# A decoder block's start reordered: small rows in ScalarE's queue, GpSimd's powers beside PSUM reads, the second row block turned in one go

## The chip, the cores and the metric

The kernel runs on one core of a Trainium2 chip. A core has five engines with a queue of instructions each: TensorE (PE in the profile; its weight loads are PEld), VectorE (DVE), ScalarE (ACT), GpSimd (POOL) and SyncE (SP), which only issues transfers here. Times are device microseconds (us) of one execution.

## The reference, cut to what matters

One layer over 512 tokens with 2048 features, all in float32:

```
h = rmsnorm(x, g_mix);  z = h @ w_in        # [conv B|C|V, attn Q|K|V, forget logits, two gates]
conv branch, forgetting attention, gated merge, x = x + merged @ w_mix_out
h = rmsnorm(x, g_mlp);  x = x + relu(h @ w_ff1)**2 @ w_ff2
out = rmsnorm(x, g_final)

rmsnorm(x, g) = x * rsqrt(mean(x*x) + 1e-6) * g
```

The change touches only the very start: the first `rmsnorm` and the first two of the products that make z.

## The kernel before, in words

**Products.** Every large product is done by a Strassen-like scheme on 2 x 2 blocks with seven block products, named A11, A12, S1 to S4 and A22. Each float32 operand is split into a high part (`high_of`, line 110, ScalarE, rounded to a 32-bit format that TensorE takes at full rate) and a low part (`low_of`, line 113, VectorE, the difference of the two). A block product is high x high, low x high and high x low: in `mm_rows` the lines 183, 185 and 187, in `mm_cols` the lines 164, 166 and 168. Classes of columns of w_in are `Group`s; `ahead` (through `load`, line 221) sends for a quarter of their weights, 1 MB, into one of four slots x0 to x3. `gV0` makes the first 256 columns x 2 of V, `heads[1]` (called `keys`) the first two heads' keys and queries.

**The start.** The 512 rows of x come in four blocks of 128 (`load_rows`, line 605). The sum of squares of a row is made by ScalarE (`squares`, line 487), and its power -1/2 by GpSimd (lines 483 and 623). Then the block is turned so that features lie on the partitions. For blocks 1 and 2 `turn` (line 525) does it with a matrix product whose other operand is the identity times the row factor (`dgs`, lines 654 and 668); even feature chunks make A11, odd ones A12. VectorE reads the result from PSUM and multiplies it by g_mix (`gained`, line 533). Blocks 3 and 4 are scaled in place by their factors (lines 694 and 695) and turned in pairs by `turn_both` (line 541) and `gained_both` (lines 549 and 551). The vectors g_mix, g_mlp, b_gate and conv_w come as small rows (`rows`, lines 635 and 637), are transposed on TensorE (line 649) and copied to `cols` (line 655); `rows` uses the slot x3. TensorE is fed small products that nobody reads (`stay_awake`, line 611) while it has nothing else.

**What sets the order.** Where `strict[0]` is true, `tied` holds an instruction behind the one written before it on its engine, so the start runs in the written order on each engine; with `strict[0]` false again (line 708) a planner places instructions by priority and by its own estimate of when operands are ready. A tile's slot is given on when its last reader is done. The order of TensorE's work in the start is: fillers, transposition of the small rows, fillers, block 1 turned (even, odd), V's A11 for block 1, block 2's even half turned, V's A12 for block 1, block 2's odd half turned, V's A11 and A12 for block 2, the pair-wise turning of blocks 3 and 4, then the keys.

Of the kernel before, what the change touches and what calls it, by code (L numbers as in the profile page):

```python
# [8 lines left out]
F32 = mybir.dt.float32  # L9
F32R = mybir.dt.float32r  # L10
BF16 = mybir.dt.bfloat16
AF = mybir.ActivationFunctionType
ALU = mybir.AluOpType
AX = mybir.AxisListType

P = 128
S = 512
D = 2048
KT = D // P
# [3 lines left out]
CT = CW // P  # L23
# [3 lines left out]
EPS = 1e-6  # L27
# [18 lines left out]
def tile_hybrid_block(ctx: ExitStack, tc, x, g_mix, w_in, b_f, b_gate, conv_w, w_conv_out,  # L46
                      w_attn_out, w_mix_out, g_mlp, w_ff1, w_ff2, g_final, out):
    nc = tc.nc
    x, out = x[0], out[0]
# [4 lines left out]
    stat = ctx.enter_context(tc.tile_pool(name="stat", bufs=2))  # L54
# [8 lines left out]
    def bank(i, name):  # L63
        return psum.tile([P, S], F32, tag=f"p{i}", name=name)
# [24 lines left out]
    ident = const.tile([P, P], F32, name="ident")  # L89
    mhalf = const.tile([P, 1], F32, name="mhalf")  # L90
# [12 lines left out]
    def tied(i):  # L103

        if strict[0]:
            tc.keep_in_program_order(i)
        return i

    def high_of(src, hi):
        return tied(nc.scalar.activation(out=hi, in_=src, func=AF.Copy))  # L110

    def low_of(src, hi, lo):
        return tied(nc.vector.tensor_tensor(out=lo, in0=src, in1=hi.bitcast(F32), op=ALU.subtract))  # L113
# [365 lines left out]
    def rstd_of(part, both=False):  # L479
        v = stat.tile([P, 1], F32, tag="v", name="v")  # L480
        tied(nc.vector.tensor_reduce(out=v, in_=part, axis=AX.X, op=ALU.add))
        r = stat.tile([P, 1], F32, tag="r", name="r")
        nc.gpsimd.tensor_tensor(out=r, in0=v, in1=mhalf, op=ALU.pow)
        return (v, r) if both else r
# [82 lines left out]
    xin = [xp[t // 2][:, t % 2] for t in range(NT)]  # L567

    Q1 = Quarters(px, gmixT)

    def store_v(c0, w):
        def put(i, j, v):
            c = c0 + j * w
            n = min(w, AW - c)
            nc.gpsimd.dma_start(out=v_d[2 * i:2 * i + 2, :, c:c + n].rearrange("t p c -> p t c"), in_=v[:, :, :n])
            if n < w:
                add(fl[:, 2 * i:2 * i + 2, :], v[:, :, n:], bf.unsqueeze(1).to_broadcast([P, 2, NH]))
        return put
# [8 lines left out]
    gV0 = Group(w_in, COL_AV, COL_AV + VW, VW, Q1.moving, mm_rows, ((4,), (3,), (6,), (7,)), store_v(0, VW))  # L587

    def kq(hp, banks):
        return Group(w_in, COL_K + hp * HS, COL_Q + hp * HS, HS, Q1.moving, mm_cols, banks, store_kq(hp), QSCALE,  # L590
                     extra={"S3": "first"})
# [8 lines left out]
    heads = [gV0] + [kq(hp, ((a,), (3,), (6,), (7,))) for hp, a in enumerate((0, 1, 2, 5))]  # L600

    def load_rows(t, n, queues):
        w = D // n
        for i in range(n):
            tied(queues[i % len(queues)].dma_start(out=xin[t][:, i * w:(i + 1) * w],
                                                   in_=x[t * P:(t + 1) * P, i * w:(i + 1) * w]))

    def stay_awake(n):

        for i in range(n):  # L610
            tied(nc.tensor.matmul(awake[:, :P], ident, ident, start=True, stop=True))

    def squares(t, n):

        w = D // n
        for i in range(n):
            tied(square_part(xin[t][:, i * w:(i + 1) * w], ss1[:, t, i:i + 1], junk[:, i * w:(i + 1) * w]))

    def factor_of(t):

        v, r = (stat.tile([P, 1], F32, tag=f"{k}2", name=k) for k in "vr")
        nc.gpsimd.tensor_tensor(out=v, in0=ss1[:, t, 0:1], in1=ss1[:, t, 4:5], op=ALU.add)
        nc.gpsimd.tensor_tensor(out=r, in0=v, in1=mhalf, op=ALU.pow)
        return r

    both = pair(6, F32, "junk")
# [1 line left out]
    dgs = [both[:, 0, t * P:(t + 1) * P] for t in range(2)]  # L628
    ss1 = const.tile([P, NT, 5], F32, name="ss1")
    nc.vector.memset(ss1[:, :, 4:5], EPS)  # L630
    strict[0] = True
    rows = main.tile([NV, P], F32, tag="x3", name="rows")
    r0 = 0
    for src, n in ((g_mix[0], KT), (g_mlp[0], KT), (b_gate[0], 2 * KT)):
        tied(nc.gpsimd.dma_start(out=rows[r0:r0 + n, :], in_=src.rearrange("(k p) -> k p", p=P)))
        r0 += n
    tied(nc.gpsimd.dma_start(out=rows[r0:r0 + 3 * CT, :], in_=conv_w[0].rearrange("j (k p) -> (j k) p", p=P)))

    load_rows(0, 4, (nc.sync, nc.scalar))
    tied(nc.scalar.activation(out=warm, in_=warm, func=AF.Square))  # L640
    gV0.ahead(0, 0)
    load_rows(1, 2, (nc.sync,))
    gV0.ahead(1, 0)
    load_rows(2, 1, (nc.sync,))
    heads[1].ahead(0, 0)
    load_rows(3, 1, (nc.sync,))
    awake, pv = bank(3, "awake"), bank(7, "pv")
    stay_awake(12)
    tied(nc.tensor.transpose(pv[:, :NV], rows, ident[:NV, :NV]))
    stay_awake(6)  # L650
    heads[1].ahead(1, 0)

    squares(0, 4)
    tied(nc.vector.tensor_scalar(out=dgs[0], in0=ident, scalar1=rstd_of(ss1[:, 0, :]), scalar2=None, op0=ALU.mult))
    tied(nc.vector.tensor_copy(cols, pv[:, :NV]))
    even, odd = Q1.turn(0, 0, (0, 1)), Q1.turn(0, 1, (2, 5))
    hi1, lo1 = parts([P, KT // 2, VW])
# [3 lines left out]
    A11, A12 = (Q1.cut(n, 0) for n in ("A11", "A12"))  # L661
    high_of(*A11[:2])
    squares(1, 1)
    Q1.gained(0, 1, 0, odd[0])
    low_of(*A11)
    Q1.gained(0, 1, 1, odd[1])
    high_of(*A12[:2])
    tied(nc.scalar.activation(out=dgs[1], in_=ident, func=AF.Copy, scale=factor_of(1)))
    for h in range(2):
        qs = slice(h * KT // 4, (h + 1) * KT // 4)  # L670
        low_of(gV0.X[0, 0][:, qs], hi1[:, qs], lo1[:, qs])
    gV0.a, b = gV0.acc("a"), gV0.acc("b")
    mm_rows(gV0.a, Q1.moving("A11"), hi1, lo1, True, blocks=(0,))
    even = Q1.turn(1, 0, (6, 7))
    hi2, lo2 = parts([P, KT // 2, VW])
    high_of(gV0.X[1, 0], hi2)
    low_of(*A12)
    low_of(gV0.X[1, 0], hi2, lo2)
    mm_rows(b, Q1.moving("A12"), hi2, lo2, True, blocks=(0,))
    odd = Q1.turn(1, 1, (0, 1))  # L680
    squares(2, 1)
    for n in range(2):
        Q1.gained(1, 0, n, even[n])
    A11, A12 = (Q1.cut(n, 1) for n in ("A11", "A12"))
    high_of(*A11[:2])
    for n in range(2):
        Q1.gained(1, 1, n, odd[n])
    high_of(*A12[:2])
    low_of(*A11)
    low_of(*A12)  # L690
    mm_rows(gV0.a, Q1.moving("A11"), hi1, lo1, True, blocks=(1,))
    mm_rows(b, Q1.moving("A12"), hi2, lo2, True, blocks=(1,))
    squares(3, 1)
    tied(nc.vector.tensor_scalar(out=xin[2], in0=xin[2], scalar1=factor_of(2), scalar2=None, op0=ALU.mult))
    tied(nc.scalar.activation(out=xin[3], in_=xin[3], func=AF.Copy, scale=factor_of(3)))
    tied(nc.gpsimd.dma_start(out=bf, in_=b_f.to_broadcast([P, NH])))
    keys = heads[1]
    keys.ready["A11"] = hi3, lo3 = keys.places()
# [48 lines left out]
    for t in range(NT):  # L747
# [3 lines left out]
                            op0=ALU.mult)  # L751
# [22 lines left out]
    for b in range(3):  # L774
        nc.scalar.activation(out=sel[32 * b:32 * b + NH, :, :], in_=identb[0:NH, 0:NH].unsqueeze(2).to_broadcast([NH, NH, P]),
                             func=AF.Copy, scale=warm[0:NH, :])
# [119 lines left out]
    n = 0  # L896
# [253 lines left out]
    n = turns[0] + 1  # L1150
# [497 lines left out]
```

## Time and profile before

| what | us |
|---|---|
| median of 3 runs | 2447.67 |
| the runs | 2450.6, 2443.35, 2447.67 |
| the profiled execution | 2449.19 |
| its span, first to last instruction | 2447.5 |

In the profile, a line of a timeline has the start in us from the span's start, the duration (of a merged group, from its first start to its last end), the engine, the line of the kernel, the operation, output and input by the program's names, the shapes and the count; in brackets stands the idle time of the engine before it and what ended it. An engine name with q (SPq) is its queue, where transfers are issued. A float32 product of the fillers and of the turnings leaves two records each. A table of stretches has one row per stretch with the busy time of each engine, the clock that TensorE was granted as a share of the full one, and the share of the transfer engines' time that was used.

### The profile page before, as it was taken

The page shows a single profiled execution, that of the slowest core. Times are in us where ns is not written, and L with a number is a line of the kernel's source. Part 1 is how long each engine was busy: PE and PEld are TensorE (multiplying, and loading weights), DVE is VectorE, ACT ScalarE, POOL GpSimd, SP SyncE. Part 2 cuts the span into 40 slices and gives each one's busy share as a digit, 9 for nine tenths or more (in the row PEclk, how much of TensorE's full clock was granted, in tenths as well). Part 3 has the DMA queues.
Part 4 walks back from the last instruction along what each step waited for, and adds up shares of the span by engine and source line. Part 5 has one row for each costly group of instructions (what it writes and reads, how often), then busy time and mean ns, then how long its engine had stood idle before and what let it go on. Part 6 is the DMA issues. An engine that isn't in the chain of part 4 may idle for free.

```text
span 2447.5 us, 41525 instructions
## 1 busy us (share of the span) xinstructions
PE 2412.4 (99%) x17804; PEld 2268.2 (93%) x17804; DVE 2042.7 (83%) x1711; ACT 1206.3 (49%) x1232; POOL 281.3 (11%) x453
## 2 busy tenths in 40 slices
PE   8999999999999999999999999999999999999998
PEld 8999899999999999899999999999997888888886
DVE  6987777788888778888889898898978888889898
ACT  6444433344555445355656666666655333333334
POOL 1100000111121111113300000000011001100000
PEclk9999999999999999999999999999999999999999
DMA  7564544445656664657855655646587576655763
GB/s 251 168 194 148 153 135 148 141 145 178 206 169 210 209 221 151 228 156 257 302 194 180 229 196 201 234 175 229 199 303 274 168 243 228 236 193 178 248 226 101
DMA packets 283785, 489.87 MB, mean 200 GB/s; under 512 B 11669, under 2 KB 195057, under 8 KB 283217
## 3 DMA queue, kind: packets, MB, share of 16 engines
q1 hardware_dynamic: 232624, 278.48, 36.2%
q0 software_dynamic: 50112, 207.17, 22.8%
q8 instruction: 139, 2.28, 0.4%
q10 hardware_dynamic: 864, 1.57, 0.2%
q14 instruction: 46, 0.37, 0.0%
HBM read 377.60 MB, written 109.05 MB: 199 GB/s over the span
## 4 chain that ended last, share of the span: by engine, by line
PE 88%; DVE 5%; DMA 3%; issue 2%; ACT 1%; POOL 1%; DVEq 0%; SPq 0%; POOLq 0%; ACTq 0%
PE a L168 6%; PE a L164 6%; PE a L166 6%; PE a L185 5%; PE a L183 5%; PE a L187 5%; PE d L164 5%; PE d L168 5%; PE d L166 5%; PE c L164 4%; PE c L166 4%; PE c L168 4%; PE d L187 3%; PE d L185 3%; PE d L183 3%; PE b L168 2%
## 5 line engine op out<-in xcount | busy, mean ns | idle before, releaser
L110 ACT ACTIVATE th<-x 128x2048 fp32r<-128x2048 f32 (+1 forms) x280 | 537.4, 1920 | 516.3 <-DVE x L124 174.8
L113 DVE TENSOR_TENSOR tl<-x,th 128x2048 fp32r<-128x2048 f32 (+2 forms) x281 | 638.8, 2279 | 164.5 <-ACT th L110 149.4
L124 DVE TENSOR_TENSOR x<-x,x 128x2048 f32<-128x2048 f32 (+1 forms) x160 | 365.6, 2285 | 24.1 <-DMA x<-in_w_in_dram 20.2
L110 ACT ACTIVATE th<-y 128x2048 fp32r<-128x2048 f32 (+1 forms) x109 | 185.7, 1704 | 273.8 <-PE a L185 138.6
L113 DVE TENSOR_TENSOR tl<-y,th 128x2048 fp32r<-128x2048 f32 (+1 forms) x109 | 218.9, 2013 | 29.5 <-ACT th L110 27.9
L183 PE MATMUL a<-th,us 128*128 128x512 f32 x512 | 199.3, 389 | 1.9 <-ACT th L110 1.9
L185 PE MATMUL a<-th,us 128*128 128x512 f32 x512 | 199.2, 389 | 0.0
L164 PE MATMUL c<-S,th 128*128 128x256 f32 x848 | 196.3, 277 | 0.6 <-ACT th L110 0.6
L166 PE MATMUL c<-S,th 128*128 128x256 f32 x848 | 195.9, 277 | 0.0
L164 PE MATMUL a<-S,th 128*128 128x256 f32 x784 | 182.3, 278 | 0.8 <-ACT th L110 0.8
L166 PE MATMUL a<-S,th 128*128 128x256 f32 x784 | 180.8, 276 | 0.0
L164 PEld LDWEIGHTS c<-S,th 128*128 128x128 f32 x848 | 159.3, 188 | 1.0 <-ACT th L110 0.7
L166 PEld LDWEIGHTS c<-S,th 128*128 128x128 f32 x848 | 159.3, 188 | 0.0
L164 PEld LDWEIGHTS a<-S,th 128*128 128x128 f32 x784 | 147.2, 188 | 1.0 <-ACT th L110 1.0
L166 PEld LDWEIGHTS a<-S,th 128*128 128x128 f32 x784 | 147.3, 188 | 0.0
L187 PE MATMUL a<-tl,us 128*128 128x512 f32 x512 | 136.9, 389 | 0.6 <-DVE tl L113 0.6
L166 PE MATMUL b<-A,th 128*128 128x256 f32 x544 | 126.9, 278 | 0.0
L164 PE MATMUL b<-A,th 128*128 128x256 f32 x544 | 126.9, 278 | 0.0
L164 PE MATMUL a<-A,th 128*128 128x256 f32 x544 | 126.5, 278 | 0.0
L166 PE MATMUL a<-A,th 128*128 128x256 f32 x544 | 126.4, 277 | 0.0
L164 PE MATMUL d<-S,th 128*128 128x256 f32 x544 | 126.3, 278 | 0.0
L166 PE MATMUL d<-S,th 128*128 128x256 f32 x544 | 125.8, 277 | 0.0
(393 smaller groups left out, 6081.6 us busy)
## 6 DMA issues: line engine op xcount, KB each, us to landing
x<-in_w_in_dram SPq DMA_DIRECT2D x86, 1024.0 KB, 5.9
y<-in_w_ff_dram SPq DMA_DIRECT2D x64, 1024.0 KB, 7.6
x<-in_w_ff_dram SPq DMA_DIRECT2D x60, 1024.0 KB, 8.3
us<-s_d POOLq DMA_DIRECT2D x48, 1024.0 KB, 9.4
s_d<-rh POOLq DMA_DIRECT2D x32, 896.0 KB, 5.1
s_d<-r POOLq DMA_DIRECT2D x32, 896.0 KB, 5.6
x<-in_w_mix_out_dram SPq DMA_DIRECT2D x17, 1024.0 KB, 6.7
g_d<-o POOLq DMA_DIRECT2D x32, 256.0 KB, 2.9
```

Source lines behind the costliest of these rows:

```text
L110: return tied(nc.scalar.activation(out=hi, in_=src, func=AF.Copy))
L113: return tied(nc.vector.tensor_tensor(out=lo, in0=src, in1=hi.bitcast(F32), op=ALU.subtract))
L124: return nc.vector.tensor_tensor(out=out, in0=a, in1=b, op=ALU.subtract)
L164: nc.tensor.matmul(o, hi[:, q, js], Sh, start=first and q == 0 and j == 0, stop=False, skip_group_check=True)
L166: nc.tensor.matmul(o, hi[:, q, js], Sl, start=False, stop=False, skip_group_check=True)
L168: nc.tensor.matmul(o, lo[:, q, js], Sh, start=False, stop=q == nq - 1, skip_group_check=True)
L183: tied(nc.tensor.matmul(o, Sh, hi[:, q, :], start=begin and q == 0, stop=False, skip_group_check=True))
L185: tied(nc.tensor.matmul(o, Sl, hi[:, q, :], start=False, stop=False, skip_group_check=True))
L187: tied(nc.tensor.matmul(o, Sh, lo[:, q, :], start=False, stop=q == nq - 1, skip_group_check=True))
```

## The change

- The first block's rows are issued by SyncE alone, in four pieces, and first of all; the small rows are issued by ScalarE instead of GpSimd.
- The rows of block 4 are issued ahead of the keys' weights, and both quarters of the keys' weights follow directly.
- One filler more stands behind the transposition of the small rows.
- Row factors: the addition of epsilon moves from GpSimd to VectorE (`mean_of`), and GpSimd does the power alone (`factor`), written so that VectorE's next instruction reads PSUM. Block 1's power is now tied too.
- In VectorE's order half of the low part of V's first weights moves ahead of block 2's factor, and block 1's second odd gain behind it; ScalarE makes block 2's factor matrix before A12's high part.
- Block 2's odd half is turned directly behind its even half, ahead of V's A12 for block 1.
- Block 2's even gains move ahead of the low part of V's second weights; its A11 is split completely before its odd gains; the squares of block 4 move ahead of them, and the factors and scalings of blocks 3 and 4 ahead of the last split.

```diff
--- before.py
+++ after.py
@@ -616,11 +616,16 @@
         for i in range(n):
             tied(square_part(xin[t][:, i * w:(i + 1) * w], ss1[:, t, i:i + 1], junk[:, i * w:(i + 1) * w]))
 
-    def factor_of(t):
-
-        v, r = (stat.tile([P, 1], F32, tag=f"{k}2", name=k) for k in "vr")
-        nc.gpsimd.tensor_tensor(out=v, in0=ss1[:, t, 0:1], in1=ss1[:, t, 4:5], op=ALU.add)
-        nc.gpsimd.tensor_tensor(out=r, in0=v, in1=mhalf, op=ALU.pow)
+    def mean_of(t):
+
+        v = stat.tile([P, 1], F32, tag="vf", name="v", bufs=4)
+        tied(nc.vector.tensor_scalar(out=v, in0=ss1[:, t, 0:1], scalar1=EPS, scalar2=None, op0=ALU.add))
+        return v
+
+    def factor(v):
+
+        r = stat.tile([P, 1], F32, tag="rf", name="r", bufs=4)
+        tied(nc.gpsimd.tensor_tensor(out=r, in0=v, in1=mhalf, op=ALU.pow))
         return r
 
     both = pair(6, F32, "junk")
@@ -629,29 +634,30 @@
     ss1 = const.tile([P, NT, 5], F32, name="ss1")
     nc.vector.memset(ss1[:, :, 4:5], EPS)
     strict[0] = True
+    load_rows(0, 4, (nc.sync,))
     rows = main.tile([NV, P], F32, tag="x3", name="rows")
     r0 = 0
     for src, n in ((g_mix[0], KT), (g_mlp[0], KT), (b_gate[0], 2 * KT)):
-        tied(nc.gpsimd.dma_start(out=rows[r0:r0 + n, :], in_=src.rearrange("(k p) -> k p", p=P)))
+        tied(nc.scalar.dma_start(out=rows[r0:r0 + n, :], in_=src.rearrange("(k p) -> k p", p=P)))
         r0 += n
-    tied(nc.gpsimd.dma_start(out=rows[r0:r0 + 3 * CT, :], in_=conv_w[0].rearrange("j (k p) -> (j k) p", p=P)))
-
-    load_rows(0, 4, (nc.sync, nc.scalar))
+    tied(nc.scalar.dma_start(out=rows[r0:r0 + 3 * CT, :], in_=conv_w[0].rearrange("j (k p) -> (j k) p", p=P)))
     tied(nc.scalar.activation(out=warm, in_=warm, func=AF.Square))
     gV0.ahead(0, 0)
     load_rows(1, 2, (nc.sync,))
     gV0.ahead(1, 0)
     load_rows(2, 1, (nc.sync,))
+    load_rows(3, 1, (nc.sync,))
     heads[1].ahead(0, 0)
-    load_rows(3, 1, (nc.sync,))
+    heads[1].ahead(1, 0)
     awake, pv = bank(3, "awake"), bank(7, "pv")
     stay_awake(12)
     tied(nc.tensor.transpose(pv[:, :NV], rows, ident[:NV, :NV]))
-    stay_awake(6)
-    heads[1].ahead(1, 0)
+    stay_awake(7)
 
     squares(0, 4)
-    tied(nc.vector.tensor_scalar(out=dgs[0], in0=ident, scalar1=rstd_of(ss1[:, 0, :]), scalar2=None, op0=ALU.mult))
+    part = stat.tile([P, 1], F32, tag="vf", name="part", bufs=4)
+    tied(nc.vector.tensor_reduce(out=part, in_=ss1[:, 0, :], axis=AX.X, op=ALU.add))
+    tied(nc.vector.tensor_scalar(out=dgs[0], in0=ident, scalar1=factor(part), scalar2=None, op0=ALU.mult))
     tied(nc.vector.tensor_copy(cols, pv[:, :NV]))
     even, odd = Q1.turn(0, 0, (0, 1)), Q1.turn(0, 1, (2, 5))
     hi1, lo1 = parts([P, KT // 2, VW])
@@ -663,36 +669,38 @@
     squares(1, 1)
     Q1.gained(0, 1, 0, odd[0])
     low_of(*A11)
+    qs, rest = slice(0, KT // 4), slice(KT // 4, KT // 2)
+    low_of(gV0.X[0, 0][:, qs], hi1[:, qs], lo1[:, qs])
+    v = mean_of(1)
     Q1.gained(0, 1, 1, odd[1])
+    tied(nc.scalar.activation(out=dgs[1], in_=ident, func=AF.Copy, scale=factor(v)))
     high_of(*A12[:2])
-    tied(nc.scalar.activation(out=dgs[1], in_=ident, func=AF.Copy, scale=factor_of(1)))
-    for h in range(2):
-        qs = slice(h * KT // 4, (h + 1) * KT // 4)
-        low_of(gV0.X[0, 0][:, qs], hi1[:, qs], lo1[:, qs])
+    low_of(gV0.X[0, 0][:, rest], hi1[:, rest], lo1[:, rest])
     gV0.a, b = gV0.acc("a"), gV0.acc("b")
     mm_rows(gV0.a, Q1.moving("A11"), hi1, lo1, True, blocks=(0,))
-    even = Q1.turn(1, 0, (6, 7))
+    even, odd = Q1.turn(1, 0, (6, 7)), Q1.turn(1, 1, (0, 1))
     hi2, lo2 = parts([P, KT // 2, VW])
     high_of(gV0.X[1, 0], hi2)
     low_of(*A12)
+    for n in range(2):
+        Q1.gained(1, 0, n, even[n])
     low_of(gV0.X[1, 0], hi2, lo2)
     mm_rows(b, Q1.moving("A12"), hi2, lo2, True, blocks=(0,))
-    odd = Q1.turn(1, 1, (0, 1))
     squares(2, 1)
-    for n in range(2):
-        Q1.gained(1, 0, n, even[n])
     A11, A12 = (Q1.cut(n, 1) for n in ("A11", "A12"))
     high_of(*A11[:2])
+    low_of(*A11)
+    squares(3, 1)
+    r2 = factor(mean_of(2))
     for n in range(2):
         Q1.gained(1, 1, n, odd[n])
+    r3 = factor(mean_of(3))
     high_of(*A12[:2])
-    low_of(*A11)
+    tied(nc.vector.tensor_scalar(out=xin[2], in0=xin[2], scalar1=r2, scalar2=None, op0=ALU.mult))
+    tied(nc.scalar.activation(out=xin[3], in_=xin[3], func=AF.Copy, scale=r3))
     low_of(*A12)
     mm_rows(gV0.a, Q1.moving("A11"), hi1, lo1, True, blocks=(1,))
     mm_rows(b, Q1.moving("A12"), hi2, lo2, True, blocks=(1,))
-    squares(3, 1)
-    tied(nc.vector.tensor_scalar(out=xin[2], in0=xin[2], scalar1=factor_of(2), scalar2=None, op0=ALU.mult))
-    tied(nc.scalar.activation(out=xin[3], in_=xin[3], func=AF.Copy, scale=factor_of(3)))
     tied(nc.gpsimd.dma_start(out=bf, in_=b_f.to_broadcast([P, NH])))
     keys = heads[1]
     keys.ready["A11"] = hi3, lo3 = keys.places()
```

## The prediction

> **What bounds the kernel now.** I read the page's first and fourth parts, then the start by timeline, the waits of SP's queue, and a table of stretches laid on the grid on which the granted clock changes.
>
> ```profile
> PE 2412.4 (99%) x17804; PEld 2268.2 (93%) x17804; DVE 2042.7 (83%) x1711; ACT 1206.3 (49%) x1232; POOL 281.3 (11%) x453
> PE 88%; DVE 5%; DMA 3%; issue 2%; ACT 1%; POOL 1%; DVEq 0%; SPq 0%; POOLq 0%; ACTq 0%
> ```
>
> TensorE is busy for 99% of the span and holds 88% of the chain that ended last. Every edit lies before the pair-wise turning of row blocks 3 and 4 (line 541), so the question is how much earlier that stage starts, and whether what follows moves with it.
>
> ```profile
> 5.79:9.20 3.41, 1.53 (x14) 1.37 (x14) 0.75 (x4) 1.90 (x6) 0.83 (x2) 1.00 1.08 362
> 9.20:12.61 3.41, 3.41 (x19) 3.41 (x18) 0.19 (x1) 1.91 (x1) 0.00 (x0) 0.50 1.03 386
> 16.02:19.43 3.41, 2.53 (x19) 2.33 (x19) 3.41 (x5) 2.20 (x3) 2.12 (x2) 1.00 1.05 361
> 19.43:22.85 3.42, 3.30 (x26) 3.10 (x27) 1.87 (x2) 3.02 (x3) 0.37 (x1) 1.00 1.03 397
> 26.27:29.68 3.41, 1.62 (x14) 1.42 (x13) 2.91 (x4) 1.87 (x3) 0.00 (x0) 1.00 1.10 348
> 29.68:33.09 3.41, 3.41 (x18) 3.41 (x17) 2.02 (x2) 2.14 (x3) 1.64 (x3) 0.50 0.53 168
> 36.50:88.00 51.50, 51.45 (x439) 51.25 (x439) 50.87 (x34) 31.94 (x27) 6.08 (x8) 1.00 0.60 185
> 1183.39:1186.80 3.41, 3.41 (x18) 3.41 (x17) 3.41 (x3) 1.60 (x2) 2.40 (x5) 0.50 0.94 248
> 1224.35:1227.76 3.41, 1.47 (x13) 1.27 (x12) 1.52 (x1) 1.80 (x1) 0.00 (x0) 1.00 0.52 213
> 1227.76:1231.18 3.42, 3.26 (x28) 3.26 (x29) 3.28 (x3) 1.36 (x3) 0.00 (x0) 1.00 0.02 5
> ```
>
> The columns are length, then busy time (instructions) of PE, PEld, DVE, ACT and POOL, granted clock, DMA share, GB/s. In 5.79 to 9.20 PE is busy for only 1.53 us, and in the next 3.41 us its clock is 0.50; the same happens after 26.27 to 29.68 (1.62 us). The stretch with 2.53 us is followed by a clock of 1.00. From 36.5 to 88 us PE works 51.45 of 51.50 us, so a start gained before 36.5 is carried on, not absorbed by a later idle time.
>
> ```profile
> 8.38 0.27 PE L649 MATMUL pv<-ident,rows 88*128 88x88 f32 x1 [1.88 <-DMA rows<-in_conv_w_dram]
> 10.46 4.76 PE L525 MATMUL ptr<-junk,xn 128*128 128x128 f32 x32
> 29.34 0.38 PE L185 MATMUL a<-th,A 128*128 128x256 f32 x1 [1.79 <-DVE A L113]
> 35.77 0.96 PE b L187 x8
> 36.56 3.66 PE L541 MATMUL ptr<-ident,xn 128*128 128x128 f32 x32
> ```
>
> The row transposition at 8.38 waited 1.88 us for the small rows; block 1's turning starts at 10.46 and runs at half clock; the product at 29.34 waited 1.79 us for VectorE's A11; the pair-wise turning begins at 36.56. That last number is the one I move. A turning of 16 records costs 3.66 / 2 = 1.83 us, a product of 24 records 24 x 0.96 / 8 = 2.9 us.
>
> **The change part by part.** First the queues.
>
> ```profile
> 0.81 0.90 ACTq L605 DMA_DIRECT2D xn<-in_x_dram  x2
> 0.81 0.85 SPq L605 DMA_DIRECT2D xn<-in_x_dram  x2
> 1.72 0.43 SPq L221 DMA_DIRECT2D x<-in_w_in_dram  x1
> 1.73 1.28 ACT L640 ACT_TABLE_LOAD   x1 [1.73 <-PEq L1634]
> 5.06 0.63 ACT L487 ACTIVATE junk<-xn 128x512 f32<-128x512 f32 x1 [1.82 <-DMA xn<-in_x_dram]
> 5.22 2.94 SPq L605 DMA_DIRECT2D xn<-in_x_dram  x1
> SPq L605 <- DMA xn<-in_x_dram: 1.1, 1, 1.1
> DMA to landing us min/median/max: 4.2/9.2/14.2
> ```
>
> Small rows in ScalarE's queue: ACT issues four loads of 0.90 / 2 = 0.45 us instead of two, ends at 2.6 and loads its table until 3.9. The one-column activation behind it (less than the 0.41 of a 128-column one below) is over by 4.3, still 0.7 us ahead of the first square at 5.06. That is the cover; with it gone each issue would delay the squares by 0.45 us. GpSimd loses four issues; its next work on the path, at 7.97, waited 4.14 us for VectorE anyway. The last small row goes out at 2.2; with the 4.2 us of the quickest x load it lands by 6.4, where the transposition had to wait until 8.38. The twelve fillers end 1.88 before that, at 6.5. With seven fillers more (14 records at 0.12 us, 1.7 us) PE is busy to about 8.4.
>
> SP now issues four chunks, 0.43 us each, and V's first weights follow at 2.5 instead of 1.72. Here the change adds a wait. At 5.22 SP's ninth hardware-queue load went out only when the first x chunk had landed (1.1 us of waiting; ACT's square starts on that chunk at 5.06). I read this as eight landing counters in turn. With four row loads added, V's first weights become the ninth, and wait for the first load to land; behind them in SP's queue stand block 2's rows and every later weight. Lower end: nothing, if a small row holds that counter, lands early, and the DMA engines are still moving x. Upper end: 3.3 us (5.03 less 1.72). I take 0.3 us, near the lower end: the engines are the limit, and x keeps them occupied to about 5 us; both ends stay in the range. Rows ahead of the keys' weights: block 4's rows move up one 1 MB transfer, from 9.17 + 14.2 = 23.4 to about 20.6, and the keys' weights land about 2.6 us later; ScalarE touches those only after scaling block 4, so this costs nothing unless it came 5 us later. Keys' second weights wait for the slot of the small rows, which the transposition frees near 6.8; SP is then still issuing block 3's rows (to 5.22 + 2.94 = 8.2 before).
>
> Now the walk, with these prices:
>
> ```profile
> 7.72 0.16 DVE L481 TENSOR_REDUCE v<-ss 128x1 f32<-128x5 f32 x1 [6.21 <-ACT junk L487]
> 7.97 0.57 POOL L483 TENSOR_TENSOR r<-v,mhalf 128x1 f32<-128x1 f32 x1 [4.14 <-DVE v L481]
> 8.57 0.31 DVE L654 TENSOR_SCALAR junk<-ident,r 128x128 f32<-128x128 f32 x1 [0.56 <-POOL r L483]
> 9.78 1.91 ACT L110 ACTIVATE th<-x 128x2048 fp32r<-128x2048 f32 x1 [2.09 <-DMA x<-in_w_in_dram]
> 13.48 0.69 DVE L533 TENSOR_TENSOR h<-ptr,cols 128x512 f32<-128x512 f32 x1 [0.36 <-PE ptr L525]
> 14.20 1.06 ACT L110 ACTIVATE A<-h 128x1024 fp32r<-128x1024 f32 x1 [2.51 <-DVE h L533]
> 15.17 1.90 ACT L487 ACTIVATE junk<-xn 128x2048 f32<-128x2048 f32 x1
> 17.04 2.35 DVE L113 TENSOR_TENSOR tl<-x,th 128x1024 fp32r<-128x1024 f32 x2
> 17.24 1.06 POOL L622 TENSOR_TENSOR v<-ss 128x1 f32<-128x1 f32 x1 [8.44 <-ACT junk L487]
> 18.38 1.42 POOL L623 TENSOR_TENSOR r<-v,mhalf 128x1 f32<-128x1 f32 x1
> 19.83 0.41 ACT L668 ACTIVATE junk<-ident,r 128x128 f32<-128x128 f32 x1 [1.62 <-POOL r L623]
> 22.07 2.29 DVE L113 TENSOR_TENSOR tl<-x,th 128x2048 fp32r<-128x2048 f32 x1 [1.55 <-ACT th L110]
> 24.49 0.55 POOL L623 TENSOR_TENSOR r<-v,mhalf 128x1 f32<-128x1 f32 x1
> 30.42 1.28 DVE L694 TENSOR_SCALAR xn<-xn,r 128x2048 f32<-128x2048 f32 x1
> 32.41 2.01 ACT L695 ACTIVATE xn<-xn,r 128x2048 f32<-128x2048 f32 x1 [1.27 <-POOL r L623]
> ```
>
> Block 1's factor is unchanged: power at 7.97, diagonal ready at 8.57 + 0.31 = 8.9. PE is there by then, so turning starts at 8.9 instead of 10.46 and, unthrottled, its 32 records end at 12.6. The first weights land at 9.78 + 0.3 = 10.1; ScalarE's high part (1.91) ends at 12.0, A11's (1.06) at 13.0 (before 15.26), block 2's squares at 15.0 (2.07 from start to the releasing of GpSimd, rows at 15.17 and 17.24).
>
> VectorE then takes A11's low part (2.35 / 2, say 1.2) to 14.3, half the weights' low part to 15.5, and the addition of the epsilon. That addition waits on VectorE now, with a gain, the rest of the low part and so PE behind it; the squares end 0.5 us before VectorE comes. The trace has no VectorE addition of one column; bounds are nothing and GpSimd's 0.57, and I take 0.1, near VectorE's sum of five columns (0.16). The two GpSimd instructions of the old factor cost 1.06 + 1.42 = 2.5 us beside a two-input VectorE subtraction (17.04); one power beside a PSUM read cost 0.55 (24.49). So the factor is ready at 16.2, the diagonal (0.41) at 16.65, where before it was 20.24. In that time VectorE reads one PSUM bank (0.69, to 16.2) and finishes the weights' low part at 17.4. PE, which waited at 13.0 for A11's low part and at about 16.7 for this one, ends the first product at 17.9 and turns block 2 at once: even half, odd half, 21.6. The three products after it need 8.7 us.
>
> VectorE is the engine to watch there: A12's low part to 18.9, block 2's first gain at 19.0 (8 records and the end of the last, 1.1 us after the turning begins), the second to 20.7, the second weights' low part (2.29) to 23.0, A11's to 24.2, an addition and two gains to 25.6, an addition and block 3's scaling (1.28) to 27.0, A12's low part to 28.2. PE's fourth product begins at 27.4, waits from 27.6 to 28.2 and ends at 30.9. ScalarE squares blocks 3 and 4 at 19.6 to 24.7 and scales block 4 (2.01) by about 29.2, so the pair-wise turning starts at 30.9: 5.7 us earlier. What is late next is VectorE's low part of A12, and behind it nothing until the turning. GpSimd's third power meets block 4's path only: between 0.55 and 1.42 us, hidden by the 1.7 us that block 4 is early.
>
> Of the 5.7 us, two half-clock stretches are 2 x 3.41 x 0.5 = 3.4 and shorter idling 2.3. The new gaps are 0.4, 0.9, 0.7 and 0.6 us, at most some 1.4 us in one stretch, so PE stays busy for 2.0 of 3.41 us, above the 1.62 that lost the clock and below the proven 2.53; I take it as safe. The Trainium skill, "TensorE: Matmul & The Clock Gate", section "Why this matters for your kernels", says only idle gaps above about 3 us bring the clock down. By that the old gaps of 1.9 us would have been harmless and the gain 2.3 us, 2446.9; this trace disagrees, with a clock of 0.50 after 1.88 us.
>
> The profiled execution took 2449.19 us, 1.69 more than its span, and lies 1.5 above the median of the runs, 2447.67. So 2449.2 - 5.7 = **2443.5 us**, 0.17% under that median. About 0.3% (7.3 us) is what a measurement of this kernel can tell from no change.
>
> **The rivals.** (a) *The grid.* Everything after the start moves by 5.7 us against the 3.41-us grid. The gap before 1183.39 lost a stretch, the one in 1224.35 to 1227.76, with PE busy for 1.47 us, did not. If two more such gaps lose theirs, 2443.5 + 3.4 = 2446.9. The same page, Part 1, says this window runs freely and does not start with the kernel, which the three runs' spread of 7 us would fit and no row here shows.
>
> (b) *No gaps left.* PE works without a pause from 8.9: four turnings and four products, 4 x 1.83 + 4 x 2.9 = 18.9, end at 27.8, a gain of 8.8: 2440.4, and 2438.7 if the stretch at 1183 is not lost either. It needs ScalarE and VectorE to be two to three us earlier than my walk; for it: the row at 9.78 shows ScalarE waiting for weights, which could land sooner with all of x in one queue. Against it: VectorE's chain above is nearly closed.
>
> (c) *The ninth load.* V's first weights are 3.3 us late, all after them too; 3.0 more than counted: 2446.5. The change then does little of what it says.
>
> (d) *Slower.* Only the start is tied to the written order; what follows is placed by the planner. From 36.5 to 88 VectorE is busy for 50.87 of 51.50 us beside a full PE. If the earlier start makes the planner put sums of the activations ahead of weights' low parts there, each such 2.29-us instruction delays PE by that much. From the third (6.9 us) the gain is gone; four and one lost clock stretch give 2449.2 - 5.7 + 9.2 + 1.7 = 2454.4, five 2456.7. For it: no slack in that stretch. Against: all engines move together, so the planner sees the same distances.
>
> **How the numbers follow.** Forecast 0.43 (its own range 2441 to 2446), (a) 0.13, (b) 0.22, (c) 0.09, (d) 0.13. Below 2440.3 lie four fifths of (b) and a small tail of the forecast: faster 0.25. Above 2455 lies two thirds of (d): slower 0.09. The rest, 0.66, is within 0.3%. The range 2439 to 2449 leaves out (d) and the low third of (b).
>
> **What would show it.** Row transposition before 7 us and no 0.50 clock in the first 40 us; block 1's turning near 8.9; the high part of V's first weights at 9.8 to 10.4 (13 would be (c)); block 2's power near 0.55 us; both turnings of block 2 back to back from about 18; the pair-wise turning at 30 to 32; 36 to 90 unchanged but for the shift. A pair-wise turning at 31 with a time not lower would speak for (a) or (d), and the page's groups after 40 us would tell which.

## The result, and the profile after

| | before, us | changed, us | ratio, 95% interval |
|---|---|---|---|
| median | 2445.94 (14 runs, 2442.87 to 2451.07) | 2442.52 (14 runs, 2439.40 to 2446.52) | 0.9984 (0.9976 to 0.9992) |
| the same, timed again later | 2445.75 (21 runs, 2440.82 to 2452.35) | 2442.23 (11 runs, 2439.03 to 2445.45) | 0.9984 (0.9975 to 0.9993) |
| the profiled execution, its span | 2449.19, 2447.5 | 2440.97, 2439.3 | |

By the medians the change saves 3.4 us of 2446, 0.14% (0.16% by the ratio). The interval leaves out 1, so there is a gain, but it lies inside the 0.3% that counts as no change. The forecast was 2443.5 us. The time, and that it counts as no change, are as forecast; two terms of the sum behind them are not, and the time that it was counted from was high.

The first and the fourth part of the page say the same as before: TensorE all but full, with 86% of the chain where it had 88%.

```profile
PE 2407.8 (99%) x17806; PEld 2263.8 (93%) x17806; DVE 2043.1 (84%) x1714; ACT 1204.5 (49%) x1232; POOL 277.2 (11%) x446
PE 86%; DVE 6%; DMA 3%; issue 3%; ACT 2%; POOL 1%; DVEq 0%; SPq 0%; POOLq 0%; ACTq 0%
```

So the start has to be read again. This is the timeline of the changed kernel, cut to the rows that answer to the forecast's steps (start, duration, engine, line; lines from 616 on have moved: 622 is the addition of epsilon, 628 the power, 654 the transposition of the small rows, 660 and 676 the factor matrices, 700 the scaling of block 4).

```profile
4.40 0.38 SPq L221 DMA_DIRECT2D x<-in_w_in_dram  x1
6.16 0.26 PE L654 MATMUL pv<-ident,rows 88*128 88x88 f32 x1
8.76 3.84 PE L525 MATMUL ptr<-junk,xn 128*128 128x128 f32 x32 [0.75 <-DVE junk L660]
11.13 1.91 ACT L110 ACTIVATE th<-x 128x2048 fp32r<-128x2048 f32 x1 [3.59 <-DMA x<-in_w_in_dram]
14.04 0.39 PE L183 MATMUL a<-th,A 128*128 128x256 f32 x1 [1.44 <-ACT A L110]
15.30 0.39 PE L185 MATMUL a<-th,A 128*128 128x256 f32 x1 [0.87 <-DVE A L113]
16.30 0.14 DVE L622 TENSOR_SCALAR v<-ss 128x1 f32<-128x1 f32 x1
16.53 0.55 POOL L628 TENSOR_TENSOR r<-v,mhalf 128x1 f32<-128x1 f32 x1 [7.90 <-DVE v L622]
17.11 0.40 ACT L676 ACTIVATE junk<-ident,r 128x128 f32<-128x128 f32 x1 [1.18 <-POOL r L628]
19.64 3.73 PE L525 MATMUL ptr<-junk,xn 128*128 128x128 f32 x32
27.05 1.52 POOL L628 TENSOR_TENSOR r<-v,mhalf 128x1 f32<-128x1 f32 x1 [0.71 <-DVE v L622]
28.61 2.01 ACT L700 ACTIVATE xn<-xn,r 128x2048 f32<-128x2048 f32 x1 [0.60 <-POOL r L628]
32.21 3.84 PE L541 MATMUL ptr<-ident,xn 128*128 128x128 f32 x32
```

The small rows no longer hold TensorE up (6.16, no wait; before 8.38), and block 1's turning starts at 8.76 in place of 10.46. Then V's first weights come late: ScalarE waits 3.59 us for them, and TensorE 1.44 us for ScalarE. The pair-wise turning starts at 32.21 in place of 36.56. That start is the mark by which the runs below are compared: 4.35 us earlier, where 5.7 were forecast.

The waits of SP's queue up to 15 us name what held the weights (us in all, times, longest):

```profile
SPq L221 <- DMA rows<-in_g_mix_dram: 1.8, 1, 1.8
```

The chain of work, followed back through the start (start, duration, what), begins there:

```profile
4.40 6.71 DMA x<-in_w_in_dram
11.11 0.02 issue
11.13 1.91 ACT th L110
```

And this is the table of stretches, with the columns of the forecast's (length, busy time and count of PE, PEld, DVE, ACT, POOL, granted clock, DMA share, GB/s):

```profile
12.21:15.62 3.41, 1.09 (x7) 0.70 (x6) 1.82 (x3) 3.41 (x3) 0.00 (x0) 1.00 1.10 384
15.62:19.03 3.41, 3.41 (x18) 3.41 (x17) 3.09 (x5) 2.23 (x5) 0.55 (x1) 0.50 1.03 423
32.15:83.65 51.50, 50.14 (x438) 49.53 (x438) 50.62 (x34) 32.35 (x28) 6.06 (x8) 1.00 0.60 187
35.80:79.40 43.60, 43.60 (x387) 43.59 (x385) 43.53 (x25) 25.94 (x19) 5.17 (x7) 1.00 0.69 214
```

The half-clock stretches that stood at 9.20 and 29.68 before are gone, but there is a new one at 15.62, behind a stretch in which TensorE worked 1.09 of 3.41 us. The last two rows are for later: the stretch behind the mark.

### The profile page after: what moved, and what is told of

It is laid out like the page before. It is cut to its first block, busy times and chain, and to the rows that moved or that the text cites. A ratio compares the mean times of both kernels' runs of the same rounds, so it can differ in the third digit from the quotient of the medians.

```text
span 2439.3 us, 41519 instructions
## 1 busy us (share of the span) xinstructions
PE 2407.8 (99%) x17806; PEld 2263.8 (93%) x17806; DVE 2043.1 (84%) x1714; ACT 1204.5 (49%) x1232; POOL 277.2 (11%) x446
## 3 DMA queue, kind: packets, MB, share of 16 engines
q10 hardware_dynamic: 724, 1.09, 0.1%
## 4 chain that ended last, share of the span: by engine, by line
PE 86%; DVE 6%; DMA 3%; issue 3%; ACT 2%; POOL 1%; DVEq 0%; SPq 0%; POOLq 0%; ACTq 0%
PE a L168 6%; PE a L164 6%; PE a L166 6%; PE d L164 5%; PE d L166 5%; PE d L168 5%; PE a L185 5%; PE a L183 5%; PE a L187 5%; PE c L164 4%; PE c L166 4%; PE c L168 4%; PE d L187 3%; PE d L183 3%; PE d L185 3%
```

## The experiments

The time of one execution says little here, since runs of one kernel spread over 5 to 12 us. The start of the pair-wise turning says more: it can be read to 0.01 us in each trace. Between executions of one kernel it moves by more than that: the two traces of the changed kernel have 32.21 and 31.96, the two of the kernel with three pieces 30.25 and 30.28. Every other kernel has one trace. The table has that mark, the start of ScalarE's high part of V's first weights, where half-clock stretches begin (up to 40 us, and from there to 2400 us), the start of the thousandth matrix instruction behind the mark, and the time of the profiled execution.

| kernel | weights' high part | half clock, start | mark | 1000 further | half clock, later | time, us |
|---|---|---|---|---|---|---|
| before | 9.78 | 9.20, 29.68 | 36.56 | 152.87 | 1183.4 | 2449.19 |
| changed | 11.13 | 15.62 | 32.21 | 148.58 | none | 2440.97 |
| e1, three pieces | 9.69 | none | 30.25 | 146.62 | 1220.0 | 2440.80 |
| e2, fillers | 11.11 | none | 31.37 | 147.73 | none | 2439.35 |
| e3, power beside subtraction | 11.17 | 15.7 | 32.25 | 148.63 | none | 2442.72 |
| e4, odd half late | 11.07 | 16.2 | 33.56 | 149.94 | none | 2440.95 |
| e5, keys' weights first | 11.08 | 15.4 | 33.08 | 149.46 | 1223.8, 1834.7 | 2445.80 |
| e6, queues alone | 11.43 | none | 34.10 | 151.28 | 1222.9, 1833.9 | 2445.55 |
| e7 (e1 again) | 9.74 | none | 30.28 | 146.96 | none | 2438.25 |
| e8 (changed again) | 11.70 | none | 31.96 | 148.33 | 1222.6, 1833.6 | 2444.73 |
| e9, conv_w by GpSimd | 10.53 | none | 30.78 | 147.14 | 1077.7 | 2441.82 |

What a kernel has gained at the mark it still has a thousand matrix instructions further (the two lie 116.3 or 116.4 us apart in nine of the eleven traces, 116.7 in e7 and 117.2 in e6). Much of what the times differ by beyond the mark goes with the two columns on the clock.

**The ninth load.** Theory: V's first weights are the ninth load of the hardware queues and wait for the first one's landing counter. With block 1's rows in three pieces they are the eighth.

```diff
-    load_rows(0, 4, (nc.sync,))
+    for c0, c1 in ((0, 512), (512, 1024), (1024, 2048)):
+        tied(nc.sync.dma_start(out=xin[0][:, c0:c1], in_=x[:P, c0:c1]))
```

> Block 1's rows go out in three pieces (512, 512 and 1024 columns) instead of four, all else as in the changed kernel. Theory: V's first weights land at 11.1 us because their load, the ninth on the hardware queues, waits for the first small row (issue at 4.40). Now they are the seventh or eighth: issue at 1.8 to 2.7, landing near 9.8, ScalarE's high part starts there instead of at 11.13, TensorE's gap before the first product shrinks from 1.44 to about 0.4 us, no half clock in the first 40 us, and the pair-wise turning starts at 30.8 to 31.3 instead of 32.21. Rival: the weights are late because all of x shares one queue with them; then they still land at about 11 us and the pair-wise turning stays at 32.2.

The timeline of the kernel with three pieces:

```profile
2.19 0.43 SPq L221 DMA_DIRECT2D x<-in_w_in_dram  x1
3.98 0.82 SPq L605 DMA_DIRECT2D xn<-in_x_dram  x2
9.69 1.91 ACT L110 ACTIVATE th<-x 128x2048 fp32r<-128x2048 f32 x1 [1.91 <-DMA x<-in_w_in_dram]
12.92 0.39 PE L183 MATMUL a<-th,A 128*128 128x256 f32 x1
30.25 3.84 PE L541 MATMUL ptr<-ident,xn 128*128 128x128 f32 x32
```

The weights go out without a wait at 2.19, and the load behind them, now the ninth, waits instead, for the same small row; the waits of SP's queue in this kernel:

```profile
SPq L605 <- DMA rows<-in_g_mix_dram: 1.3, 1, 1.3
```

The gap of 1.44 us in TensorE is gone, the half clock with it, and the mark stands at 30.25: 6.3 us earlier than before, and earlier than the 30.8 to 31.3 that were expected. Three pieces could have helped for another reason, that larger pieces of x land sooner. So in a later run the pieces stayed four and one small row went back to GpSimd's own queue, which makes the weights the eighth load too:

```diff
-    tied(nc.scalar.dma_start(out=rows[r0:r0 + 3 * CT, :], ...
+    tied(nc.gpsimd.dma_start(out=rows[r0:r0 + 3 * CT, :], ...
```

> The changed kernel with one thing undone: the fourth small row, conv_w, is issued by GpSimd again. Block 1's rows keep their four pieces, so that only the number of loads ahead of V's first weights in the hardware queues falls, from eight to seven. My theory: the wait of V's first weights comes from their being the ninth load, and the pieces of x have nothing to do with it. Then SyncE issues them at about 2.6 us, right behind the four pieces (1.81 us from 0.81), instead of 4.40; ScalarE's high part of them starts at 9.6 to 10.0, as with three pieces (9.69 and 9.74), and the pair-wise turning at 30.2 to 30.6 with no half-clock stretch, or some 0.85 us later with one. The row transposition, which now waits for GpSimd's load, may come at 6.8 to 8.4; if it is later than 7.0 block 1's turning moves by at most the same. Rival: three pieces helped because fewer and larger pieces of x land sooner; then the issue stays at 4.40 or the high part at 11.1 or later, and the pair-wise turning at 31.4 to 32.2.

```profile
2.67 0.43 SPq L221 DMA_DIRECT2D x<-in_w_in_dram  x1
7.54 0.63 ACT L487 ACTIVATE junk<-xn 128x512 f32<-128x512 f32 x1 [0.60 <-DMA xn<-in_x_dram]
9.51 3.84 PE L525 MATMUL ptr<-junk,xn 128*128 128x128 f32 x32 [1.21 <-DVE junk L660]
10.53 1.91 ACT L110 ACTIVATE th<-x 128x2048 fp32r<-128x2048 f32 x1 [2.27 <-DMA x<-in_w_in_dram]
30.78 3.83 PE L541 MATMUL ptr<-ident,xn 128*128 128x128 f32 x32
```

The issue at 2.67 is what the count says: the wait comes from the number of loads, whatever is in them. The second half of the expectation missed: the weights were touched at 10.53, not at 9.6 to 10.0, and block 1's last square waited for x until 7.54, so that its turning came at 9.51 (8.76 in the changed kernel). The mark came at 30.78, just behind the expected 30.2 to 30.6. Here 1.7 us of earlier issue gave 0.6 us of earlier landing. It would fit that loads on their way share the transfer engines, but no run shows it, and 0.6 us is no more than the spread: seven traces with the issue at 4.20 to 4.40 us have the weights touched at 11.07 to 11.70. Why three pieces lose less, no run tells.

**The half clock.** To part it from the late weights, twelve records of filler work were put into the gap, everything else unchanged.

```diff
     even, odd = Q1.turn(0, 0, (0, 1)), Q1.turn(0, 1, (2, 5))
+    stay_awake(6)
```

> Six more fillers behind the turning of block 1, in TensorE's gap from 12.6 to 14.0 us; all else as in the changed kernel. Theory: the half clock at 15.6 to 19.0 us follows from that gap; with it filled the clock stays at 1.00, the first product ends near 18.7 instead of 19.6, and the pair-wise turning starts at 31.0 to 31.5 instead of 32.21, though no operand comes sooner. Rival: VectorE's low parts set the pace and the half clock was hidden; then the pair-wise turning stays within 0.3 us of 32.2.

```profile
12.29 1.50 PE L611 MATMUL awake<-ident 128*128 128x128 f32 x12
14.02 0.39 PE L183 MATMUL a<-th,A 128*128 128x256 f32 x1 [0.23 <-ACT A L110]
31.37 3.83 PE L541 MATMUL ptr<-ident,xn 128*128 128x128 f32 x32
```

The first product starts where it did (14.02 against 14.04), the clock stays whole, and the mark comes at 31.37. So the half clock costs 32.21 - 31.37 = 0.84 us at the mark, half of the 1.7 that it takes from TensorE, and the late weights cost 31.37 - 30.25 = 1.12 us. That second difference is one between two kernels, but two more traces in the new order without a half clock in the start (e9 and e8) bear it out: with the weights' high part at 10.53, 11.11 and 11.70 the mark is at 30.78, 31.37 and 31.96, one for one; the step down to 9.69 brings only another 0.53 us.

**The power beside the subtraction.** VectorE's order is put back so that the power runs beside a two-input subtraction again, as one GpSimd instruction.

```diff
-    low_of(gV0.X[0, 0][:, qs], hi1[:, qs], lo1[:, qs])
-    v = mean_of(1)
     Q1.gained(0, 1, 1, odd[1])
+    v = mean_of(1)
+    low_of(gV0.X[0, 0][:, qs], hi1[:, qs], lo1[:, qs])
```

> In VectorE's order block 1's second odd gain moves ahead of block 2's addition of epsilon, and both halves of the weights' low part behind it, so that GpSimd's power for block 2 runs beside a two-input subtraction instead of a PSUM read; all else as in the changed kernel. Theory: the power takes 1.4 us or more instead of 0.55 (as the old kernel's took 1.42), the diagonal is ready about 0.5 us later than at 17.5, and the pair-wise turning starts 0.4 to 1 us later than 32.21. Rival: GpSimd's old 2.5 us were two instructions behind ScalarE's squares and not a collision; then the power stays at 0.5 to 0.6 us and nothing moves by more than 0.3 us.

```profile
16.02 2.35 DVE L113 TENSOR_TENSOR tl<-x,th 128x1024 fp32r<-128x1024 f32 x2
16.19 1.46 POOL L628 TENSOR_TENSOR r<-v,mhalf 128x1 f32<-128x1 f32 x1 [7.71 <-DVE v L622]
17.68 0.40 ACT L676 ACTIVATE junk<-ident,r 128x128 f32<-128x128 f32 x1 [1.76 <-POOL r L628]
```

The power takes 1.46 us instead of 0.55, as it should by the theory, but the mark stays (32.25), where 0.4 to 1 us was expected. The factor matrix is ready at 18.08, and TensorE is busy with the first product until 19.6, so the slow power is hidden. Moving this power beside the PSUM read is worth nothing at the mark here. The first product runs at half clock in this trace; at full clock it ended at 18.8 (the kernel with fillers), which would still leave 0.7 us of cover. The addition, which the change takes from GpSimd as well, was not given back alone in any run.

**The turning in one go.** The odd half goes back behind V's A12 for block 1.

```diff
-    even, odd = Q1.turn(1, 0, (6, 7)), Q1.turn(1, 1, (0, 1))
+    even = Q1.turn(1, 0, (6, 7))
...
     mm_rows(b, Q1.moving("A12"), hi2, lo2, True, blocks=(0,))
+    odd = Q1.turn(1, 1, (0, 1))
```

> Block 2's odd half is turned behind V's A12 for block 1 again, as before the change; all else as in the changed kernel. Theory: that product now follows the even half at once and waits about 1 us for the low part of V's second weights, which before the change and without this order VectorE finishes near 24.5 us; the odd gains then come 1 us later and the pair-wise turning starts 0.8 to 1.5 us after 32.21. Rival: VectorE's chain alone sets the pace; then the pair-wise turning moves by less than 0.3 us and this part of the change is worth nothing.

```profile
24.52 1.22 PE L187 MATMUL b<-tl,A 128*128 128x256 f32 x8 [1.08 <-DVE tl L113]
33.56 2.63 PE L541 MATMUL ptr<-ident,xn 128*128 128x128 f32 x21
```

The mark moves back by 1.35 us. TensorE comes to the low part of V's second weights 1.08 us before it is made; in the changed kernel the odd half is turned in that time.

**Rows ahead of keys' weights.** The keys' first weights go out ahead of block 4's rows again.

```diff
-    load_rows(3, 1, (nc.sync,))
     heads[1].ahead(0, 0)
+    load_rows(3, 1, (nc.sync,))
```

> Block 4's rows are sent for behind the keys' first weights again, as before the change; all else as in the changed kernel. Theory: they land near 23.4 us instead of 20.4, ScalarE's squares of block 4 start at about 23.4 instead of 23.32, and the pair-wise turning moves by less than 0.3 us from 32.21: this part of the change is worth nothing while the weights of V are late. Rival: a transfer of rows behind one of weights lands 1.5 us later still; then the squares start near 25, VectorE's addition for block 4 waits, and the pair-wise turning comes 1 to 1.5 us later.

```profile
25.64 1.92 ACT L487 ACTIVATE junk<-xn 128x2048 f32<-128x2048 f32 x1 [2.27 <-DMA xn<-in_x_dram]
27.68 0.15 DVE L622 TENSOR_SCALAR v<-ss 128x1 f32<-128x1 f32 x1 [0.81 <-ACT junk L487]
33.08 3.19 PE L541 MATMUL ptr<-ident,xn 128*128 128x128 f32 x26
```

My theory held this to be worth nothing; the rival won. In the new order the squares of block 4 stand at 23.3, before that block would have landed, and VectorE's addition of epsilon is behind them: 0.81 us of wait, 33.08 - 32.21 = 0.87 at the mark, a little under the 1 to 1.5 us of the rival.

**The queues alone.** The kernel before with only block 1's rows in SP's queue and the small rows in ScalarE's.

```diff
+    load_rows(0, 4, (nc.sync,))
...
-        tied(nc.gpsimd.dma_start(out=rows[r0:r0 + n, :], ...
+        tied(nc.scalar.dma_start(out=rows[r0:r0 + n, :], ...
...
-    tied(nc.gpsimd.dma_start(out=rows[r0:r0 + 3 * CT, :], ...
+    tied(nc.scalar.dma_start(out=rows[r0:r0 + 3 * CT, :], ...
-    load_rows(0, 4, (nc.sync, nc.scalar))
```

> The kernel before with the queue part alone: block 1's rows by SyncE in four pieces, the small rows by ScalarE; orders, powers and the later loads as before. Theory: the small rows land by 6.2 us and block 1's turning starts near 8.8 instead of 10.46 without a half clock behind it, but V's first weights become the ninth load and land at about 11.1 instead of 9.76, so that the pair-wise turning starts only 1 to 2 us earlier than the 36.56 of the kernel before: 34.6 to 35.6. Rival: the queue part carries the whole gain; then it starts at 32 to 33.

```profile
11.43 1.91 ACT L110 ACTIVATE th<-x 128x2048 fp32r<-128x2048 f32 x1 [3.89 <-DMA x<-in_w_in_dram]
34.10 1.91 PE L541 MATMUL ptr<-ident,xn 128*128 128x128 f32 x16
```

The mark is at 34.10, 2.46 us earlier than before: between my theory and the rival, nearer to the first. It bears the late weights as well (11.43), and its early part has no half clock. That last point needs care, as TensorE's wait for block 2's A11 is still there:

```profile
28.35 0.39 PE L185 MATMUL a<-th,A 128*128 128x256 f32 x1 [1.80 <-DVE A L113]
24.86:28.27 3.41, 1.70 (x16) 1.50 (x14) 2.49 (x3) 1.88 (x3) 0.00 (x0) 1.00 1.09 350
```

The wait is as long as before (1.80 us against 1.79), and the product behind it starts 0.99 us earlier (28.35 against 29.34). But the grid cut this gap so that its stretch has 1.70 us of work, where before had 1.62, and the clock stayed whole. So 0.99 us of the 2.46 is what the queues brought up to there; the other 1.47 comes behind that product, where before runs at half clock and this execution does not. That is the grid's doing, not the queues'; without it the mark would stand near 35.6 (an estimate: 36.56 - 0.99), the upper end of what the theory gave. Against it the kernel with fillers, also at full clock, has 31.37: 2.7 us for all the rest of the change, of which 0.3 is weights that were touched sooner (11.11).

**Is it to be had?** The kernel with three pieces and the changed kernel were timed side by side.

> The kernel of three pieces again, now timed. Its pair-wise turning started at 30.25 us, 6.3 before that of the kernel before and 2.0 before that of the changed kernel. Theory: a start gained is carried on to the end, so 2445.9 - 6.3 = 2439.6 us, with 2 us either way for the clock windows and transfers of the later stages, and about 2 us under the changed kernel timed beside it. Rival: a later stage gives the last 2 us back; then it stands within 1 us of the changed kernel, near 2442.

> The changed kernel itself, timed beside the one above on the same chip: about 2442 us, 3 to 4.5 under the kernel before, as its pair-wise turning starts 4.35 us earlier.

With three pieces: 2440.48 us (11 runs, 2438.18 to 2443.35), ratio to before 0.9979 (0.9970 to 0.9988). The changed kernel: 2442.23, 0.9984 (0.9975 to 0.9993). The medians lie 1.75 us apart, the marks in the traces of these timings 1.68 (30.28 and 31.96); the intervals overlap, so that the order of the two rests on the traces more than on the times. It is the fastest of the kernels timed over many runs, still within 0.3% of before.

The second trace of the changed kernel tells more than its time. Its timeline, and its table of stretches:

```profile
14.61 0.38 PE L183 MATMUL a<-th,A 128*128 128x256 f32 x1 [2.08 <-ACT A L110]
```

```profile
10.83:14.24 3.41, 1.71 (x16) 1.51 (x14) 1.34 (x2) 2.54 (x2) 0.00 (x0) 1.00 1.04 387
14.24:17.66 3.42, 2.17 (x16) 1.97 (x17) 3.07 (x5) 2.32 (x3) 0.55 (x1) 1.00 1.07 407
1219.18:1222.59 3.41, 1.31 (x12) 1.11 (x11) 1.37 (x2) 2.11 (x2) 0.00 (x0) 1.00 0.64 265
1222.59:1226.01 3.42, 3.42 (x17) 3.42 (x18) 3.42 (x3) 1.04 (x2) 0.00 (x0) 0.50 0.03 7
```

This execution's gap is longer than the first one's, 2.08 us against 1.44, and costs no clock. The first two rows are cut at the grid that the 0.50 stretch at 1222.59 gives, counted back in steps of 3.413 us: the grid's edge falls into the gap and splits it, and TensorE is busy for 1.71 and 2.17 us. In the first execution the edges (12.21 and 15.62) take in both of its gaps and leave 1.09. The kernel is the same; the two grids stand some 1.4 us apart (12.21 and 10.83) when counted from its first instruction. The Trainium skill, "TensorE: Matmul & The Clock Gate", section "What's actually happening" of Part 1, says that the window runs freely and isn't reset by the start of a kernel; these two traces agree.

## Why the prediction was right, and where it was not

**Right for the reason given, at a smaller size.** Only the start changed, and what it gained was carried on: at the mark 4.35 us, a thousand matrix instructions later 152.87 - 148.58 = 4.29. The medians say 3.4 and 3.5, with some 2 us to either side. 2443.5 was reached from a base of 2449.19, which lies in the upper part of before's runs: a profiled execution with three half-clock stretches in the forecast's table. The gain forecast was too large, by 1.35 us at the mark and 2.3 by the medians; the base was 1.5 us above the median known then and 3.3 above that of 14 runs. The two errors lie on opposite sides, so that the forecast came within 1.0 us of the measured 2442.52 is in part luck.

**What a half clock costs.** The forecast counted before's two half-clock stretches at 1.7 us each, 3.4 of its 5.7. At the mark the second was worth 1.47 (before against the queues alone), and the new one of the changed kernel 0.84 (fillers). Both hang on the grid of one execution, so the 4.35 us is a difference of two single executions too. The forecast's other sum, 2446.9, by which gaps of this length cost no clock, has these runs against it: the new half clock stands behind gaps of 1.44 and 0.87 us, and with the first of them filled it is gone.

**The ninth load: the term that was mis-sized.** The wait was named, its bounds were set at 0 and 3.3 us, and 0.3 was taken, "near the lower end", since x would keep the engines occupied. It cost 1.35 us at the weights (11.13 against 9.78), and 1.12 at the mark. Busy engines did not hide it: the issue slipped from 1.72 to 4.40, 2.7 us, and half of that was left. Rival (c) was the same mechanism at its upper end; the truth lies between.

**"I take it as safe": failed.** The walk's gaps were 0.4, 0.9, 0.7 and 0.6 us. The first became 1.44 through the weights, the second came at 0.87 as forecast, and both fell into one grid stretch: 1.09 us of work, then half a clock. It is worth 0.84 us at the mark. The late weights and this make 1.96 us against the kernel with three pieces, whose mark of 30.25 lies 0.65 us ahead of the walk's 30.9; the rest, 1.31, is what the walk missed by. Of the 0.65, up to 0.4 is weights that came sooner than the walk had them (9.69 for 10.1). So the walk itself, from the weights on, was good to a few tenths of a us.

**Small steps.** Small rows at 6.16 (before 7 forecast), block 1's turning at 8.76 (8.9), the addition of epsilon 0.14 us (0.1), block 2's power 0.55 (0.55), both turnings back to back (from 17.9 forecast, from 19.64 measured, by the two terms above), and the third power hidden as forecast, though ScalarE waited 0.60 us for it. It took 1.52 us, over the upper bound of 1.42: VectorE's next instruction there does not read PSUM but is the scaling of block 3, with one large input. The Trainium skill, "GPSIMD Engine Reference", section "1. Specifications", says that GpSimd contends with VectorE's instructions that have two SBUF inputs and with those in a mode that uses two ports. The 1.46 us beside the subtraction fits the first; whether the scaling ran in such a mode no trace shows.

**A gain without a price.** Rows ahead of the keys' weights: the forecast priced what becomes late (the keys' weights), at nothing, and gave no price to what the new order needs early. The squares of block 4 had been moved ahead as well, and with the rows behind the keys' weights the mark came 0.87 us later.

**The rivals.** (a) The grid: its mechanism exists, but in the execution and not in the kernel. The two traces of the changed kernel differ by 3.76 us in time; one has half-clock stretches at 1222.6 and 1833.6, the other has none there: 2 x 1.7 = 3.4. (b) No gaps left: it did not come true in the changed kernel. The kernel with three pieces comes nearest, with a gain of 6.3 of the 8.8 at the mark, and what it changes is what (b) asked for, V's weights sooner. That its median of 2440.48 meets the 2440.4 of (b) is luck, as that was counted from the high base. (d) The planner: it did exchange VectorE instructions in two places between 53 and 67 us, each time a Strassen sum of the activations (line 124) going ahead of a low part, and this cost TensorE nothing that the distance to before shows (4.35 at the mark and then 4.29).

**A right conclusion from a wrong bound.** From 36.5 to 88 us the forecast took TensorE to be the limit, being busy for 51.45 of 51.50 us. The same block products took less time in the changed kernel: the row 35.80:79.40 above has 387 records in 43.60 us, the table of before has the same 387 in 45.22.

```profile
39.98:85.20 45.22, 45.22 (x387) 45.22 (x386) 45.04 (x26) 27.14 (x19) 5.34 (x7) 1.00 0.66 205
```

TensorE was 1.6 us faster there at the same clock, and the gain was not kept: behind it TensorE waits, by the waits of the changed kernel from 79 to 84 us.

```profile
PE c L183 <- ACT th L110: 1.0, 1, 1.0
PE c L187 <- DVE tl L113: 0.4, 1, 0.4
```

ScalarE's high part waits for VectorE's sums, and VectorE worked almost without a pause in both kernels (50.62 and 50.87 of 51.50 us). These are the changed kernel's high part and low part for those products, and the same low part before:

```profile
78.61 1.92 ACT L110 ACTIVATE th<-x 128x2048 fp32r<-128x2048 f32 x1 [3.82 <-DVE x L124]
80.76 2.28 DVE L113 TENSOR_TENSOR tl<-x,th 128x2048 fp32r<-128x2048 f32 x1
85.04 2.29 DVE L113 TENSOR_TENSOR tl<-x,th 128x2048 fp32r<-128x2048 f32 x1
```

VectorE comes to that low part 48.5 us behind the mark in both traces (80.76 - 32.21 and 85.04 - 36.56), whatever TensorE's pace. So by these traces VectorE sets that stretch, though no run changed its load there; TensorE was just slow enough in the one trace of before to look like the limit. A start gained is carried on because VectorE starts earlier too.

## What to carry to other kernels

When a load is added to a hardware queue, count the loads that go out ahead of each transfer on the path: here the ninth waited for one of the first to land, and giving one load less (three pieces of x, not four) was worth 1.96 us at the mark, where moving one power was worth nothing. A gap that leaves TensorE under some 1.6 us of work in a 3.41-us stretch can cost the clock, and whether it does depends on where the grid falls in that execution; in the one run with filler work in the gap the clock stayed whole. So before two single traces are compared, look whether one of them escaped a half clock that its twin paid for. An engine that is busy for all of a stretch isn't yet its limit: look whether a second one is as full, before counting on either.

## What was not expected of the hardware

- The 384 products of one block stage went out every 118 ns in the trace of before and every 113 ns in the ten others, at a granted clock of 1.00 (45.22 and 43.60 us for 387 records). No run was made to find out why; it stays open.
- The busy time that loses the clock isn't a clean threshold: 1.09, 1.31, 1.53 and 1.62 us of 3.41 were followed by a clock of 0.50; 1.71 was not, and neither was 1.47 in the forecast's table (1224.35 to 1227.76 of before). Laid each on its own grid, from the first clock on record up to 2400 us, the eleven traces say together: every stretch with 1.44 us or less was followed by the half clock, none with 1.67 or more; in between 1.53 and 1.62 (both in before) were, and 1.47 (before), 1.57 (e7) and 1.59 (e2) were not.
- An issue of V's first weights that was 2.7 us later (4.40 against 1.72) brought them 1.35 us later; issues 1.7 and 2.2 us sooner than that (2.67 in e9, 2.19 in e1) brought them 0.60 and 1.44 us sooner. So in these traces a third to two thirds of a shift in issue reached the landing, while x was on its way too (a DMA share of 1.08 from 5.79 to 9.20 us in the forecast's table). The spread is large: with the issue at 4.20 to 4.40 us, seven traces have the weights touched at 11.07 to 11.70.
